# Gates, branch, output and down projections with the tokens stationary and 512 weight columns moving

## The chip, the cores and the metric

The kernel runs on one core of a Trainium2 chip. The metric is device time in microseconds (us); the figure quoted for a kernel is the median of its runs. A profile shows one execution, with the busy time of TensorE (PE, its weight loads apart as PEld), VectorE (DVE), ScalarE (ACT), GpSimd (POOL), and the queues that issue transfers (SP's above all).

## The reference

One encoder layer on 256 tokens, D = 2048, in float32. `setup_inputs` only draws values; the shapes are constants.

```python
h = rmsnorm(x, mix_norm)
z = h @ w_in                  # q/kv latents, rotary key, conv v/B/C, memory query, 3 x 2048 gates
y_mla  = mla_attention(...) @ w_o_mla            # 1024 -> 2048
y_conv = (cb * dwconv_centred(cc * cv, conv_w)) @ w_out_conv   # 1024 -> 2048
y_mem  = memory_attention(...) @ w_o_mem         # 1024 -> 2048
gates  = sigmoid(g + gate_bias)                  # (256, 3, 2048)
merged = gates[0] * y_mla + gates[1] * y_conv + gates[2] * y_mem
x = x + merged @ w_o                             # 2048 -> 2048
u = dwconv_centred(rmsnorm(x, ffn_norm) @ w_up, ffn_conv_w)    # 2048 -> 2 x 5632
a, b = split(u)
x = x + (silu(a) * b) @ w_down                   # 5632 -> 2048
return rmsnorm(x, final_norm)
```

## The kernel before

Every float32 operand of a product is cut into two float32r halves: `hi` is a rounded copy (made on ACT), `lo` the remainder (a subtraction on DVE). A product is three products: hi x hi, lo x hi and hi x lo. Weights come from memory in blocks of 128 x 2048 (1 MB; `load`, three buffers `raw`, issued on SP's queue), and `halves` (lines 138 and 139) makes `hi` (three buffers) and `lo` (two buffers) of each. All activations are kept features x tokens (feature-major) as tiles of 128 features x (256 hi | 256 lo).

There are two forms of a projection.

*The narrow form* (`mm`, `acc`, lines 161 to 165) has the weights stationary: a 128 x 128 piece of `hi` with the 512 columns hi|lo of the tokens moving, then a piece of `lo` with the 256 columns hi moving. One output tile is 128 output features x 256 tokens. Over 2048 input features that is 16 matmuls with 512 columns and 16 with 256. The second half of the result is added to the first afterwards by `total` (lines 185 and 187: one copy on ACT, one addition on DVE).

*The wide form* (`values`, lines 370 to 372, and `part`, lines 734 to 736) has the tokens stationary: 128 tokens of one feature tile, with 512 columns of `hi`, then of `lo` moving, then the tokens' lo half with `hi` moving. Its result is tokens x features. Before the change the value projections of the two attentions and the last 512 columns of the last down projection use it.

The stages in order: latents, keys, values and the two attentions with the gated convolution; then the merge (loop over `pair`: per pair of output tiles and per branch, two gate tiles and one block with two branch tiles of 8 input tiles each, `pair` 0 to 7); the output projection with the residual (`wo`, 16 tiles, which also makes the normalised input `h2` of the FFN); and twice (`NG`) `up` for 22 tiles of both halves of the FFN, with its convolution and gate, and `down` for 16 tiles (12 in the second round), each over 22 input tiles. At the end the last 512 columns are computed in the wide form, for one half of the tokens after the other, and `finish` normalises and stores each half; for that, part of the residual is turned by TensorE (line 724) and the factors are spread over partitions by a matmul with a diagonal (line 753).

The order of the instructions on each engine is made by the framework's scheduler from the program; each engine then runs its own list strictly in that order.

Of the kernel before, what the change touches and what calls it, by code (L numbers as in the profile page):

```python
# [64 lines left out]
TAIL = 4  # L65
LEAD = 5
# [5 lines left out]
OUT_SHAPE = (2, P, KC * P)  # L72
# [4 lines left out]
def tile_kernel(ctx: ExitStack, tc: tile.TileContext, a, out):  # L77
# [21 lines left out]
    def temp(name):  # L99
        tag, bufs = {"hl": ("hl", 2), "t": ("t", 3), "s": ("s", 2), "sq": ("sq", 3)}.get(name, ("w", 8))  # L100
        return tmp.tile([P, T], F32, tag=tag, name=name, bufs=bufs)
# [528 lines left out]
    mg = [slot(f"mg{i}", F32R) for i in range(KC)]  # L630
    for pair in range(KC // 2):
        ms_ = [None, None]
        for br, (w, src) in enumerate((("woa", oa), ("woc", yc), ("wom", om))):
            gs = []
            for j in range(2):
                hi, lo = wblock()
                t = total(mm(hi, lo, 0, xs))
                nc.vector.tensor_tensor(t, t, rsb, op=ALU.mult)
                g = temp(f"g{j}")
                nc.scalar.activation(g, t, AF.Sigmoid, bias=col("gb", br * KC + 2 * pair + j))  # L640
                gs.append(g)
            hi, lo = block(a[w][pair])
            for j in range(2):
                t = total(mm(hi, lo, j * 8 * P, src))
                if br == 0:
                    ms_[j] = temp(f"mg{j}")
                    nc.vector.tensor_tensor(ms_[j], t, gs[j], op=ALU.mult)
                else:
                    nc.vector.tensor_tensor(t, t, gs[j], op=ALU.mult)
                    nc.vector.tensor_tensor(ms_[j], ms_[j], t, op=ALU.add)  # L650
        for j in range(2):
            split(mg[2 * pair + j], ms_[j])


    x2 = [slot(f"xr{i}") for i in range(KC // 2)]
    h2 = []
    fsq = temp("sq")
    for i in range(KC):
        if i % 2 == 0:
            nc.sync.dma_start(x2[i // 2], a["xT"][:, i * T : (i + 2) * T])  # L660
        hi, lo = block(a["wo"][i])
        t = total(mm(hi, lo, 0, mg))
        x = half(x2[i // 2], i % 2)
        nc.vector.tensor_tensor(x, x, t, op=ALU.add)
        d = slot(f"h2_{i}", F32R)
        split(d, x, col("ffn", i))
        h2.append(d)
        square_sum(fsq, x, i == 0)
# [4 lines left out]
    def up(c):  # L673
        ps = [mm(*block(a["wup"][2 * c + part]), 0, h2) for part in range(2)]
        if not rfb:
            rfb.append(spread(norm_factor(fsq, D, "f"), half(fb, 0)))
        ab = []
        for part in range(2):
            t = total(ps[part])
            u = temp(f"u{part}")  # L680
            nc.vector.tensor_tensor(u, t, rfb[0], op=ALU.mult)  # L681
            v = temp(f"v{part}")
            conv(u, v, "fcw", part * NFF + c, 2 * NFF)
            ab.append(v)
        s = temp("si")
        nc.scalar.activation(s, ab[0], AF.Silu)
        nc.vector.tensor_tensor(s, s, ab[1], op=ALU.mult)  # L687
        f = slot(f"f{c}", F32R)
        split(f, s)
        return f  # L690

    osq = temp("sq")
    wdn = iter(range(a["wdn"].shape[0]))

    def down(fs, tiles, last):
        n = len(fs) // 2
        for i in range(tiles):
            ps = psum()
            for b in range(2):
                hi, lo = block(a["wdn"][next(wdn)], n=n * P)  # L700
                acc(ps, hi, lo, 0, fs[b * n : (b + 1) * n], b == 0, b == 1)
            x = half(x2[i // 2], i % 2)
            nc.vector.tensor_tensor(x, x, total(ps), op=ALU.add)
            if last:
                square_sum(osq, x, i == 0)
                nc.scalar.activation(x, x, AF.Copy, scale=col("fin", i))

    ready = []
    for g in range(NG):
        fs = ready + [up(c) for c in range(g * GF + len(ready), (g + 1) * GF)]  # L710
        ready = [up((g + 1) * GF)] if g < NG - 1 else []
        last = g == NG - 1
        down(fs, KC - TAIL if last else KC, last)

    gains = slot("gains")
    nc.scalar.dma_start(gains, a["fing"])
    rows = []
    for h in range(2):  # L720
        pt = atps.tile([P, 2 * T], F32, tag="at", name="ptr")
        for c in range(TAIL):
            src = half(x2[(KC - TAIL + c) // 2], c % 2)
            nc.tensor.transpose(pt[:, c * P : (c + 1) * P], src[:, h * P : (h + 1) * P], ident)
        rows.append(slot(f"rows{h}"))
        nc.scalar.activation(rows[h], pt, AF.Copy)
    rest = tiny.tile([P, 2], F32, tag="rest", name="rest")
    nc.vector.tensor_scalar(rest, feature_sums(osq), 1.0 / D, EPS, op0=ALU.mult, op1=ALU.add)
    po = [psum() for _ in range(2)]

    def part(h, c, hi, lo):
        f = fs[c]
        fh, fl = f[:, h * P : (h + 1) * P], f[:, T + h * P : T + (h + 1) * P]
        nc.tensor.matmul(po[h], fh, hi, start=c == 0, stop=False)  # L734
        nc.tensor.matmul(po[h], fh, lo, start=False, stop=False)  # L735
        nc.tensor.matmul(po[h], fl, hi, start=False, stop=c == GF - 1)  # L736

    left = (KC - TAIL) * P

    def finish(h):  # L740
        y, junk = slot(f"y{h}"), slot("junk")
        nc.vector.tensor_tensor(y, po[h], rows[h], op=ALU.add)
        m = tiny.tile([P, 2], F32, tag="om", name="om")
        nc.scalar.activation(junk, y, AF.Square, accum_out=m[:, 0:1])
        nc.vector.tensor_scalar(
            m[:, 1:2], m[:, 0:1], 1.0 / D, rest[:, h : h + 1], op0=ALU.mult, op1=ALU.add
        )
        r = tiny.tile([P, 1], F32, tag="or", name="or")
        nc.gpsimd.tensor_tensor(r, m[:, 1:2], mhalf[:, 0:1], op=ALU.pow)
        dg = tmp.tile([P, P], F32, tag="dg", name="dg")  # L750
        nc.vector.tensor_scalar(dg, ident, r, None, op0=ALU.mult)
        ps = atps.tile([P, 2 * T], F32, tag="at", name="pso")
        spread_in = nc.tensor.matmul(ps[:, 0:P], ones, dg, start=True, stop=True)
        res = raws.tile([P, WB], F32, tag="raw", name="res")
        g = slot(f"g{h}")
        nc.vector.tensor_tensor(g, y, gains, op=ALU.mult)
        nc.scalar.activation(res[:, left:], g, AF.Copy, scale=r)
        by = ps[:, 0:P].unsqueeze(1).to_broadcast([P, 2, P])
        for i in range((KC - TAIL) // 2):
# [6 lines left out]
            elif i == 0:  # L766
                nc.sync.dma_start(out[h][:, left:], res[:, left:])
# [3 lines left out]
    for b in range(0, GF, 4):  # L771
# [137 lines left out]
```

## Time and profile before

| | |
|---|---|
| median of 3 runs | 1642.61 us (1641.99 to 1644.32) |
| profiled execution, its own time | 1642.26 us |
| its span in the profile | 1640.5 us (1.76 us of the time lie around it) |
| PE busy | 1626.7 us, 99% of the span |
| PEld / DVE / ACT busy | 88% / 69% / 51% |
| chain that ended last | PE 98% |

A duration of one matmul is longer than the distance to the next, since matmuls overlap in the array. Where the time of a sequence of matmuls is wanted, it is read as the distance from start to start.

### The profile page before, as it was taken

To read this page: it belongs to the slowest core of one execution; us is meant where nothing else is said; L and a number is where in the kernel's file an instruction comes from. 1 tells how busy PE (TensorE), PEld (TensorE's weight loads), DVE (VectorE), ACT (ScalarE), POOL (GpSimd) and SP (SyncE) were. 2 spreads that over 40 slices of the span, in tenths; PEclk is the share of its full clock that TensorE was granted. 3 is DMA by queue.
4 is the path that set the end of the run, shared out by engine and by line. 5 is a ranking of instruction groups with operands and counts; after the bars stand their busy time and mean duration, and the time that the engine had idled before them with its cause. 6 is when DMAs were issued, how large, how long until landed. Compare 5 with 4: busy or idle time off the path is not lost.

```text
span 1640.5 us, 23631 instructions
## 1 busy us (share of the span) xinstructions
PE 1626.7 (99%) x9626; PEld 1447.5 (88%) x9626; DVE 1135.0 (69%) x1535; ACT 840.0 (51%) x1118; POOL 11.6 (1%) x23
## 2 busy tenths in 40 slices
PE   9999999999999999999999999999999999999997
PEld 8998888998888888888888888888888888888886
DVE  7756768776666666666676777778555778777554
ACT  8634545554544544444455655555444455554552
POOL 0000000000000000000000000000000000000000
PEclk9999999999999999999999999999999999999999
DMA  8555445444555455555465555554556555554563
GB/s 319 205 187 183 169 149 199 155 160 170 184 186 199 180 192 193 180 194 191 178 234 205 181 197 187 182 199 160 179 192 210 198 196 181 194 190 161 184 213 116
DMA packets 52443, 308.97 MB, mean 188 GB/s; under 512 B 6000, under 2 KB 7536, under 8 KB 22256
## 3 DMA queue, kind: packets, MB, share of 16 engines
q1 hardware_dynamic: 50688, 305.82, 52.1%
q8 instruction: 76, 1.25, 0.3%
q10 hardware_dynamic: 1008, 1.12, 0.2%
q0 software_dynamic: 640, 0.52, 0.2%
q14 instruction: 31, 0.25, 0.0%
HBM read 304.17 MB, written 2.10 MB: 187 GB/s over the span
## 4 chain that ended last, share of the span: by engine, by line
PE 98%; DMA 1%; DVE 1%; issue 0%; ACTq 0%; ACT 0%; SPq 0%; POOLq 0%; POOL 0%; DVEq 0%
PE ps L161 51%; PE ps L163 29%; PE ps L165 4%; PE ps L173 2%; PE ps L174 2%; PE ps L175 2%; PE ps L371 1%; PE ps L372 1%; PE ps L370 1%; PE pss L436 1%; PE ps L734 0%; PE ps L736 0%; PE ps L735 0%; DMA raw<-in_wkv 0%; PE pst L460 0%
## 5 line engine op out<-in xcount | busy, mean ns | idle before, releaser
L139 DVE TENSOR_TENSOR lo<-raw,hi 128x2048 fp32r<-128x2048 f32 (+2 forms) x312 | 649.3, 2083 | 346.0 <-PE ps L163 272.1
L161 PE MATMUL ps<-h,hi 128*128 128x512 f32 x2520 | 606.5, 391 | 2.1 <-DVE t L187 2.1
L138 ACT ACTIVATE hi<-raw 128x2048 fp32r<-128x2048 f32 (+2 forms) x312 | 543.1, 1743 | 63.4 <-PE ps L175 18.2
L161 PEld LDWEIGHTS ps<-h,hi 128*128 128x128 f32 x2520 | 471.4, 188 | 96.5 <-DVE t L187 2.3
L163 PEld LDWEIGHTS ps<-h,lo 128*128 128x128 f32 x2688 | 345.0, 191 | 13.0
L163 PE MATMUL ps<-h,lo 128*128 128x256 f32 x2688 | 350.2, 283 | 0.0
L185 ACT ACTIVATE hl<-ps 128x256 f32<-128x256 f32 x253 | 97.5, 385 | 432.9 <-PE ps L165 425.8
L161 PE MATMUL ps<-f,hi 128*128 128x512 f32 x588 | 144.0, 391 | 0.0
L161 PEld LDWEIGHTS ps<-f,hi 128*128 128x128 f32 x588 | 108.6, 188 | 20.8
L187 DVE TENSOR_TENSOR t<-ps,hl 128x256 f32<-128x256 f32 x253 | 105.8, 418 | 8.7 <-ACT hl L185 8.7
L163 PEld LDWEIGHTS ps<-f,lo 128*128 128x128 f32 x616 | 81.4, 191 | 4.4
L163 PE MATMUL ps<-f,lo 128*128 128x256 f32 x616 | 82.8, 282 | 0.0
L544 ACT ACTIVATE v<-u,taps 128x256 f32<-128x256 f32 x88 | 44.7, 510 | 70.5 <-DVE u L681 70.5
L545 DVE SCALAR_TENSOR_TENSOR v<-u,taps,v 128x255 f32<-128x255 f32 x88 | 42.5, 484 | 48.8 <-ACT v L544 48.8
L165 PE MATMUL ps<-h,hi 128*128 128x512 f32 x168 | 66.6, 396 | 0.0
L161 PE MATMUL ps<-mg,hi 128*128 128x512 f32 x240 | 57.3, 390 | 0.0
L161 PEld LDWEIGHTS ps<-mg,hi 128*128 128x128 f32 x240 | 45.1, 188 | 9.1
L194 ACT ACTIVATE f<-si 128x256 fp32r<-128x256 f32 x44 | 18.3, 417 | 53.7 <-DVE si L687 53.7
L548 DVE SCALAR_TENSOR_TENSOR v<-u,taps,v 128x255 f32<-128x255 f32 x88 | 42.5, 484 | 3.0
L681 DVE TENSOR_TENSOR u<-t,fb 128x256 f32<-128x256 f32 x88 | 37.3, 425 | 2.9
L174 PE MATMUL ps<-m,lo 128*128 128x256 f32 x128 | 35.9, 284 | 0.0
L175 PE MATMUL ps<-m,hi 128*128 128x256 f32 x128 | 35.9, 284 | 0.0
(247 smaller groups left out, 1635.5 us busy)
## 6 DMA issues: line engine op xcount, KB each, us to landing
raw<-in_wup SPq DMA_DIRECT2D x88, 1024.0 KB, 4.8
raw<-in_win SPq DMA_DIRECT2D x83, 1024.0 KB, 4.8
raw<-in_wdn SPq DMA_DIRECT2D x56, 704.0 KB, 4.0
raw<-in_wo SPq DMA_DIRECT2D x16, 1024.0 KB, 4.8
raw<-in_wmk SPq DMA_DIRECT2D x8, 1024.0 KB, 4.9
raw<-in_wmv SPq DMA_DIRECT2D x8, 1024.0 KB, 4.8
raw<-in_woa SPq DMA_DIRECT2D x8, 1024.0 KB, 4.8
raw<-in_woc SPq DMA_DIRECT2D x8, 1024.0 KB, 4.7
```

The source lines that it names most:

```text
L138: nc.scalar.activation(hi[:, s], raw[:, s], AF.Copy)
L139: nc.vector.tensor_tensor(lo[:, s], raw[:, s], f32(hi[:, s]), op=ALU.subtract)
L161: nc.tensor.matmul(ps, hi[:, ks[k]], xs[k], start=first and k == 0, stop=False)
L163: nc.tensor.matmul(ps[:, 0:T], lo[:, ks[k]], xs[k][:, 0:T], start=False, stop=False)
L165: nc.tensor.matmul(ps, hi[:, ks[k]], xs[k], start=False, stop=True)
L174: nc.tensor.matmul(p1, lo[:, s], x[:, 0:T], start=False, stop=False)
L175: nc.tensor.matmul(p1, hi[:, s], x[:, T:], start=False, stop=stop)
L185: nc.scalar.activation(hl, ps[:, T:], AF.Copy)
L187: nc.vector.tensor_tensor(t, ps[:, 0:T], hl, op=ALU.add)
L544: nc.scalar.activation(dst, x, AF.Copy, scale=col(w, wn + wi))
L545: nc.vector.scalar_tensor_tensor(dst[:, 1:T], x[:, 0 : T - 1], col(w, wi), dst[:, 1:T], op0=ALU.mult, op1=ALU.add)
L548: nc.vector.scalar_tensor_tensor(dst[:, 0 : T - 1], x[:, 1:T], col(w, 2 * wn + wi), dst[:, 0 : T - 1], op0=ALU.mult, op1=ALU.add,)
```

## The change

The gates, the three branch projections, the output projection and both rounds of the down projection go to the wide form, by `project` and `multiply`, in groups of 512 output columns (`NW` = 4 groups); `up` stays narrow. The merged sum and the residual are then tokens x features. The merged sum must be feature-major for the output projection, and the new residual for `up`: `turned` transposes four 128-column pieces of both token halves on TensorE (8 transposes), and splits them. It is called with a delay: it is put on the list `pending` and taken from it by `flush` 12 feature tiles into a later projection (for the last group of the residual: inside the first tile of `up`). `total` falls away in the changed projections; the gate bias is read from memory, spread over the tokens, by 12 transfers issued on ACT; the mean squares are sums along a row. `finish` scales by a number per token, with no matmul. The number of buffers for `raw`, `hi` and `lo` is as before.

```diff
+    def project(src, n, xs, hook=None):
+
+        ps = [psum() for _ in range(2)]
+        per = WB // 512
+        for b in range(0, len(xs), per):
+            cnt = min(per, len(xs) - b)
+            hi, lo = block(src[n][:, b * 512 : (b + cnt) * 512], n=cnt * 512)
+            for k in range(cnt):
+                if hook is not None and b + k == len(xs) - 4:
+                    hook()
+                for h in range(2):
+                    multiply(ps[h], xs[b + k], h, hi, lo, k, b + k == 0, b + k == len(xs) - 1)
+        return ps
+
+    def multiply(ps, x, h, hi, lo, k, first, final):
+        xh, xl = x[:, h * P : (h + 1) * P], x[:, T + h * P : T + (h + 1) * P]
+        s = slice(k * 512, (k + 1) * 512)
+        nc.tensor.matmul(ps, xh, hi[:, s], start=first, stop=False)
+        nc.tensor.matmul(ps, xh, lo[:, s], start=False, stop=False)
+        nc.tensor.matmul(ps, xl, hi[:, s], start=False, stop=final)
+
+    def turned(src, dst, gain=None):
+
+        for c in range(0, 4, 2):
+            pt = psum(atps, "at")
+            for j in range(2):
+                for h in range(2):
+                    o = j * T + h * P
+                    nc.tensor.transpose(
+                        pt[:, o : o + P], src[h][:, (c + j) * P : (c + j + 1) * P], ident
+                    )
+            for j in range(2):
+                split(dst[c + j], half(pt, j), None if gain is None else col("ffn", gain + c + j))
...
-    for pair in range(KC // 2):
-        ms_ = [None, None]
+    for n in range(NW):
+        ms_ = [slot(f"m{h}") for h in range(2)]
         for br, (w, src) in enumerate((("woa", oa), ("woc", yc), ("wom", om))):
+            bias = wide("bias")
+            nc.scalar.dma_start(bias, a["gb"][:, br * D + n * 512 : br * D + (n + 1) * 512])
+            gp = project(a["wg"], br * NW + n, xs, flush)
...
+            for h in range(2):
+                g = ms_[h] if br == 0 else wide("g")
+                nc.vector.scalar_tensor_tensor(
+                    g, gp[h], rs[:, h : h + 1], bias, op0=ALU.mult, op1=ALU.add
+                )
+                nc.scalar.activation(g, g, AF.Sigmoid)
                 gs.append(g)
...
+            bp = project(a[w], n, src)
+            for h in range(2):
+                nc.vector.tensor_tensor(gs[h], bp[h], gs[h], op=ALU.mult)
+                if br:
+                    nc.vector.tensor_tensor(ms_[h], ms_[h], gs[h], op=ALU.add)
+        pending.append(lambda ms_=ms_, n=n: turned(ms_, mg[4 * n : 4 * n + 4]))
...
+        ps = project(a["wo"], n, mg, flush)
+        for h in range(2):
+            x = x2[h][n]
+            nc.vector.tensor_tensor(x, ps[h], x, op=ALU.add)
+            squares(fst, x, h, n)
...
+            ps = project(a["wdn"], g * NW + n, fs)
+            for h in range(2):
+                x = x2[h][n]
+                nc.vector.tensor_tensor(x, ps[h], x, op=ALU.add)
...
+        for i in (0, n, 1, 2):
+            s = slice(i * 512, (i + 1) * 512)
+            if i in (0, 1):
+                nc.scalar.activation(res[:, s], x2[h][i], AF.Copy, scale=r)
+            else:
+                nc.vector.tensor_scalar(res[:, s], x2[h][i], r, None, op0=ALU.mult)
+            (nc.sync if i in (n, 2) else nc.scalar).dma_start(out[h][:, s], res[:, s])
```

The built programs show where the instructions then stand. Up to the end of the gated convolution, the lists of PE, DVE and ACT are the same in both, but for the line numbers. Three places follow; the numbers behind a name tell buffers apart.

PE, out projection, from one output tile to the next before the change (`ps_7895` and `ps_7945` are the results, `mg` the merged sum):

```order
L163 MATMUL ps_7895<-mg13_4289,lo_7892 128x256
L163 MATMUL ps_7895<-mg14_4290,lo_7892 128x256
L163 MATMUL ps_7895<-mg15_4291,lo_7892 128x256
L165 MATMUL ps_7895<-mg15_4291,hi_7891 128x512
L161 MATMUL ps_7945<-mg0_4276,hi_7941 128x512
L161 MATMUL ps_7945<-mg1_4277,hi_7941 128x512
```

And after it, where the third weight block of the first group ends (`ps_6717`, `ps_6718`: first group, token halves 0 and 1; `ps_6865`, `ps_6866`: second group; `m0`, `m1`: the merged sum, tokens x features):

```order
L653 MATMUL ps_6718<-hi_6781,mg11_4287 128x512
L662 MATMUL ps_6815<-ident_85,m1_6087 128x128
L662 MATMUL ps_6824<-ident_85,m0_6086 128x128
L662 MATMUL ps_6824<-ident_85,m1_6087 128x128
L662 MATMUL ps_6824<-ident_85,m0_6086 128x128
L662 MATMUL ps_6824<-ident_85,m1_6087 128x128
L651 MATMUL ps_6865<-hi_6869,mg0_4276 128x512
L651 MATMUL ps_6866<-hi_6869,mg0_4276 128x512
L652 MATMUL ps_6865<-lo_6870,mg0_4276 128x512
```

Between the third and the fourth block of the first group now stand five transposes and most of the first block of the second group (20 matmuls, up to `mg3`), and then the fourth block with `mg12`; so two blocks are open at once.

PE, some 40 instructions on, where the fourth block of the first group ends and the rest of the second group's first block follows:

```order
L653 MATMUL ps_6718<-hi_6811,mg15_4291 128x512
L653 MATMUL ps_6865<-hi_6869,mg3_4279 128x512
L651 MATMUL ps_6866<-hi_6869,mg3_4279 128x512
L652 MATMUL ps_6866<-lo_6870,mg3_4279 128x512
L653 MATMUL ps_6866<-hi_6869,mg3_4279 128x512
L651 MATMUL ps_6865<-hi_6899,mg4_4280 128x512
L651 MATMUL ps_6866<-hi_6899,mg4_4280 128x512
L662 MATMUL ps_6963<-ident_85,x20_6690 128x128
L662 MATMUL ps_6972<-ident_85,x20_6690 128x128
L652 MATMUL ps_6865<-lo_6900,mg4_4280 128x512
```

The first matmul that needs the second block's `lo_6900` now stands eight instructions behind the end of the fourth block.

DVE, merge, before the change (`lo` is the weights' lower half, `t` a narrow tile's sum, `g` a gate):

```order
L139 TENSOR_TENSOR lo_4731<-raw_4728,hi_4730 128x2048
L187 TENSOR_TENSOR t_4667<-ps_4632,hl_4665 128x256
L638 TENSOR_TENSOR t_4667<-t_4667,rsb_567 128x256
L187 TENSOR_TENSOR t_4697<-ps_4678,hl_4695 128x256
L649 TENSOR_TENSOR t_4697<-t_4697,g0_4624 128x256
L650 TENSOR_TENSOR mg0_4411<-mg0_4411,t_4697 128x256
L139 TENSOR_TENSOR lo_4777<-raw_4774,hi_4776 128x2048
```

And after it, around the end of a gate projection (`ps_4488`, `ps_4489`) and of the branch projection behind it (`ps_4616`, `ps_4617`):

```order
L685 SCALAR_TENSOR_TENSOR g_4610<-ps_4488,xr_565,bias_4486 128x512
L143 TENSOR_TENSOR lo_4651<-raw_4648,hi_4650 128x2048
L685 SCALAR_TENSOR_TENSOR g_4613<-ps_4489,xr_565,bias_4486 128x512
L143 TENSOR_TENSOR lo_4689<-raw_4686,hi_4688 128x2048
L692 TENSOR_TENSOR g_4610<-ps_4616,g_4610 128x512
L143 TENSOR_TENSOR lo_4719<-raw_4716,hi_4718 128x2048
L692 TENSOR_TENSOR g_4613<-ps_4617,g_4613 128x512
L694 TENSOR_TENSOR m0_4292<-m0_4292,g_4610 128x512
L694 TENSOR_TENSOR m1_4293<-m1_4293,g_4613 128x512
```

An eviction that waits for the end of a projection now stands directly ahead of the `lo` of a block that PE needs later.

DVE, the end of the kernel for the first half of the tokens, before the change:

```order
L742 TENSOR_TENSOR y0_15151<-ps_14990,rows0_14976 128x512
L756 TENSOR_TENSOR g0_15164<-y0_15151,gains_14969 128x512
L745 TENSOR_SCALAR om_15154<-om_15154,rest_14985 128x1
L751 TENSOR_SCALAR dg_15159<-ident_85,or_15157 128x128
L762 TENSOR_TENSOR res_15163<-xr0_7780,pso_15161 128x256
L762 TENSOR_TENSOR res_15163<-xr1_7781,pso_15161 128x256
```

After it:

```order
L787 TENSOR_TENSOR x20_6693<-ps_13016,x20_6693 128x512
L790 TENSOR_SCALAR om_13187<-ost_7307,oe_13013 128x1
L796 TENSOR_TENSOR x20_6693<-x20_6693,gains_7311 128x512
L803 TENSOR_SCALAR res_13192<-x20_6692,or_13189 128x512
L803 TENSOR_SCALAR res_13192<-x20_6693,or_13189 128x512
```

Of six products of 128 x 256 behind the factor, two of 128 x 512 are left on DVE; two more stand on ACT, each half's last two transfers behind them.

## Rows read from the trace of the kernel before

**Rows 1.** The page's first part (busy time of each engine, share of the span, instructions) and its part 4 (the chain that ended last, by engine).

```profile
PE 1626.7 (99%) x9626; PEld 1447.5 (88%) x9626; DVE 1135.0 (69%) x1535; ACT 840.0 (51%) x1118; POOL 11.6 (1%) x23
...
PE 98%; DMA 1%; DVE 1%; issue 0%; ACTq 0%; ACT 0%; SPq 0%; POOLq 0%; POOL 0%; DVEq 0%
```

**Rows 2.** Windows by stage: start and end, length, then busy time of each engine with its instructions, granted clock of PE, busy share of the DMA engines, GB/s. In order: merge, output projection, first `down`, second `down`, last 512 columns, what follows the last matmul.

```profile
404.17:805.45 401.28, 401.28 (x2306) 354.16 (x2304) 259.48 (x312) 196.70 (x233) 0.00 (x0) 1.00 0.52 188
805.45:894.49 89.04, 89.04 (x514) 78.71 (x512) 61.73 (x81) 47.73 (x63) 0.00 (x0) 1.00 0.59 213
...
1151.48:1274.15 122.67, 122.67 (x706) 108.20 (x705) 66.49 (x68) 50.73 (x51) 0.00 (x0) 1.00 0.56 192
...
1507.95:1600.85 92.90, 92.90 (x538) 81.98 (x537) 54.55 (x62) 47.65 (x63) 0.00 (x0) 1.00 0.56 193
1600.85:1631.72 30.87, 30.87 (x139) 25.26 (x137) 15.79 (x23) 9.71 (x14) 0.55 (x1) 1.00 0.31 114
1631.72:1640.50 8.78, 0.49 (x3) 0.30 (x2) 3.96 (x10) 1.44 (x3) 0.55 (x1) 0.77 0.36 134
```

**Rows 3.** Waits of DVE and of SP's queue: engine, line, for whom, us in total, times, longest.

```profile
DVE lo L139 <- PE ps L163: 272.1, 233, 4.6
...
SPq L129 <- DVE lo L139: 1063.7, 206, 10.0
```

**Rows 4.** Timeline of PE, one narrow tile over 16 input tiles and the start of the next: start, us from first start to last end, line, operation, count.

```profile
1279.71 3.58 PE L161 MATMUL ps<-h,hi 128*128 128x512 f32 x15
1283.13 2.08 PE L163 MATMUL ps<-h,lo 128*128 128x256 f32 x16
1285.05 0.40 PE L165 MATMUL ps<-h,hi 128*128 128x512 f32 x1
1285.28 1.09 PE L161 MATMUL ps<-h,hi 128*128 128x512 f32 x4
```

**Rows 5.** Timeline of PE in the wide form (`values`): one weight block, 24 matmuls from the first row to the last but one; then four matmuls with 128 columns stand in between. The last row is from the groups by line, the weight loads of line 371: count, busy us, mean ns.

```profile
135.26 0.61 PE L370 MATMUL ps<-hi,m 128*128 128x512 f32 x2
135.72 0.39 PE L371 MATMUL ps<-lo,m 128*128 128x512 f32 x1
...
140.48 0.39 PE L372 MATMUL ps<-hi,m 128*128 128x512 f32 x1
140.70 0.61 PE L370 MATMUL ps<-hi,m 128*128 128x512 f32 x2
...
L371 PEld LDWEIGHTS ps<-lo,m 128*128 128x128 f32 x64 | 12.0, 188 | 2.4
```

**Rows 6.** Timeline of PE with four transposes (line 460) among the 15 hi matmuls of a narrow tile, and the source view of line 460 (duration ns, lowest, median, highest).

```profile
200.06 2.00 PE L161 MATMUL ps<-h,hi 128*128 128x512 f32 x8
201.90 0.27 PE L460 MATMUL pst<-ident,p 128*128 128x128 f32 x1
...
202.71 0.49 PE L460 MATMUL pst<-ident,p 128*128 128x128 f32 x3
...
203.96 2.08 PE L163 MATMUL ps<-h,lo 128*128 128x256 f32 x16
...
L460 PE MATMUL pst<-ident,p x48: 270/272/275, 186.2 to 395.7; 128*128 128x128 f32 x48
```

**Rows 7.** Timeline of PE around the two other kinds of small matmul that fall away: the column sums of the squares (line 221; one more matmul with 512 columns follows ahead of the next row) and the spreading of the factor (line 753; likewise).

```profile
1609.25 0.39 PE L735 MATMUL ps<-lo,f 128*128 128x512 f32 x1
1609.48 0.50 PE L221 MATMUL psm<-ones,sq 128*128 128x1 f32 x4
...
1610.17 0.40 PE L734 MATMUL ps<-hi,f 128*128 128x512 f32 x1
...
1627.67 0.39 PE L736 MATMUL ps<-wh,f 128*128 128x512 f32 x1
1627.89 0.38 PE L753 MATMUL pso<-dg,ones 128*128 128x128 f32 x2
...
1628.35 0.39 PE L735 MATMUL ps<-wl,f 128*128 128x512 f32 x1
```

**Rows 8.** Groups by line and shape on DVE and ACT: count, busy us, mean ns of one, idle time before them.

```profile
L139 DVE TENSOR_TENSOR lo<-raw,hi 128x2048 fp32r<-128x2048 f32 x238 | 545.3, 2291 | 253.4 <-PE ps L163 208.3 <-issue 15.3 <-PE ps L174 13.3
L742 DVE TENSOR_TENSOR y<-ps,rows 128x512 f32<-128x512 f32 x2 | 1.4, 691 | 10.6 <-PE ps L736 10.6
L138 ACT ACTIVATE hi<-raw 128x2048 fp32r<-128x2048 f32 x238 | 454.7, 1911 | 42.7 <-PE ps L175 18.2 <-PE ps L372 17.8 <-DVE lo L139 5.4
```

**Rows 9.** Timeline of all engines after the last matmul (PEld left out).

```profile
1631.33 0.39 PE L736 MATMUL ps<-wh,f 128*128 128x512 f32 x1
1631.76 0.69 DVE L742 TENSOR_TENSOR y<-ps,rows 128x512 f32<-128x512 f32 x1 [1.37 <-PE ps L736]
...
1633.53 0.55 POOL L749 TENSOR_TENSOR or<-om,mhalf 128x1 f32<-128x1 f32 x1 [6.29 <-DVE om L745]
...
1634.12 0.72 ACT L757 ACTIVATE res<-g,or 128x512 f32<-128x512 f32 x1 [0.91 <-POOL or L749]
...
1634.87 0.33 SPq L767 DMA_DIRECT2D out<-res  x1
...
1635.76 1.66 SPq L765 DMA_DIRECT2D out<-res  x3
```

**Rows 10.** DMA issues by line: count, KB each, median us from issue to landing.

```profile
raw<-in_win SPq DMA_DIRECT2D x83, 1024.0 KB, 4.8
```

More of the change, by code (lines that the diff above doesn't have):

```diff
@@ L642, in tile_kernel @@
[L642 to L652, printed above, removed]
@@ L690, in up @@
         return f
[L692 to L706, printed above, removed]
@@ L708, in tile_kernel @@
-    ready = []
+    ost = const.tile([P, 2 * NW], F32, name="ost")
+    gains = [slot("gains") for n in range(NW)]
     for g in range(NG):
-        fs = ready + [up(c) for c in range(g * GF + len(ready), (g + 1) * GF)]
-        ready = [up((g + 1) * GF)] if g < NG - 1 else []
+        fs = [up(c) for c in range(g * GF, (g + 1) * GF)]
         last = g == NG - 1
[L713 to L728, printed above, removed]
@@ L729, in tile_kernel @@
-    po = [psum() for _ in range(2)]
[L731 to L738, printed above, removed]
+        if last:
+            for n in range(NW):
+                nc.scalar.dma_start(gains[n], a["fing"][:, n * 512 : (n + 1) * 512])
@@ L740, in finish @@
+        for n in range(NW - last):
+            ps = project(a["wdn"], g * NW + n, fs)
+            for h in range(2):
+                x = x2[h][n]
+                nc.vector.tensor_tensor(x, ps[h], x, op=ALU.add)
+                if last:
+                    squares(ost, x, h, n)
+                    nc.vector.tensor_tensor(x, x, gains[n], op=ALU.mult)
+    n = NW - 1
+    rest = mean_square(ost, "o", NW - 1)
+    po = [psum() for _ in range(2)]
     def finish(h):
-        y, junk = slot(f"y{h}"), slot("junk")
@@ L803, in _rows @@
+            continue
+        for k in range(cnt):
+            hi, lo = slot("wh", F32R), slot("wl", F32R)
+            piece = raw[:, k * 512 : (k + 1) * 512]
+            nc.scalar.activation(hi, piece, AF.Copy)
+            nc.vector.tensor_tensor(lo, piece, f32(hi), op=ALU.subtract)
+            late.append((b + k, hi, lo))
+    for h in range(2):
+        for k, hi, lo in late:
+            multiply(po[h], fs[k], h, hi, lo, 0, False, k == GF - 1)
+        finish(h)
 def _rows(w):
@@ L841, in _layout @@
         order += [o_c + part * CW + i * P + r(P) for part in (0, 2, 1)]
-    for pair in range(KC // 2):
-        order += [o_g + br * D + 2 * pair * P + r(2 * P) for br in range(3)]
     h = r(HEADS)[:, None]
```

190 lines of the change are left out of this document (86 added, 104 removed).

## The prediction

> **What bounds the kernel now.** I read the page's first part and the chain of waits first: PE is busy for 99% of the span and holds 98% of the chain that ended last [rows 1]. Then the windows by stage, since the change touches some stages and not others: from the merge to the last matmul PE is busy for the whole of every stage, at the full granted clock, 2.4 GHz [rows 2]. The waits say the same from the other side: DVE stands 272.1 us waiting for PE to release a `lo` buffer, and SP's queue 1063.7 us for DVE [rows 3]. So the weights arrive and are split ahead of need, and the time is a sum over PE's instructions. What must be known is the distance from start to start of a matmul in each form, and whether PE still never waits.
>
> **What a matmul costs.** A narrow tile over 16 input tiles, 16 matmuls with 512 and 16 with 256 columns, takes 1285.28 - 1279.71 = 5.57 us [rows 4], 348 ns for a 128 x 128 piece of weights. In the wide form 24 matmuls with 512 columns take 140.70 - 135.26 = 5.44 us, 226.7 ns each [rows 5]. They cover four input tiles and four output tiles, 16 pieces, so 340 ns a piece. The columns that move are the same, 768 a piece. The 16 matmuls with 256 columns take (1285.05 - 1283.13) / 16 = 120 ns each [rows 4]. So 256 columns more make 106.7 ns, and 13.3 ns a matmul are left that don't grow with its columns. A narrow piece pays them twice and a wide one 1.5 times; the change between the two kinds in a narrow tile costs a little more. That is the gain: 8 ns a piece.
>
> The tokens' half stands still for two matmuls in turn in the wide form, but it is loaded each time: line 371 has 64 weight loads for its 64 matmuls [rows 5]. They take 188 ns, less than the 226.7 ns between matmuls, so no more comes from there.
>
> **The change part by part**, against the profiled execution (1642.26 us, of which 1640.5 are span; the median, 1642.61, is 0.35 above).
>
> *Matmuls.* Merge: 4 groups x 3 branches x (16 + 8) input tiles x 6 = 1728 matmuls, x 226.7 ns = 391.7 us, where it takes 401.28: -9.6. Output projection: 384, 87.0 us, for 89.04: -2.0. First `down`: 4 x 22 x 6 = 528, 119.7, for 122.67: -3.0. Second `down`, its first three groups: 396, 89.8, for 92.90: -3.1; the 8 transposes of line 724 stand in that window and go with it [rows 2]. The last 512 columns have that form already, `up` keeps its own. Together -17.7.
>
> *Small matmuls taken out.* Four instructions of line 221, for one column sum: from 1609.25 to 1610.17, two wide matmuls (0.45) and 0.47 us for them; two such sums fall away. The spreading of the factor in the stream: 1628.35 - 1627.67 - 0.45 = 0.23 [rows 7]. Together -1.2.
>
> *Transposes put in.* 64, eight for each of four groups of the merged sum and of the residual. Four among 15 hi matmuls make 3.90 us (200.06 to 203.96) [rows 6], where such 15 take 3.42 (1283.13 - 1279.71) [rows 4]: 0.12 us each, +7.7. The Trainium skill, "TensorE: Matmul & The Clock Gate", Part 4 (PE-mode transpose), gives about 275 ns for a transpose of 128 x 128 in a kernel. The trace agrees with that as a duration, 272 ns, but not as a price, since the next matmul starts earlier [rows 6]; at 275 ns each the 64 would cost 17.6, and nearly the whole gain would be gone.
>
> *Stalls put in.* `lo` has two buffers. In the regular course DVE writes the `lo` of the block after next when a block ends: 2.29 us [rows 8], and PE needs it 5.44 us later; an eviction of 0.69 us ahead of it leaves 2.4 us. That hides the evictions of 128 x 512 everywhere in the merge. In the half blocks that end each `down` projection, two input tiles, 2.72 us, no eviction stands between and 0.4 us are left. The one place where it does not fit is the first group of the output projection. PE must wait for the merged sum's last transposes, and the scheduler has put the second group's first block in between. When the third block ends, that block's `lo` only gets its buffer: ready after 2.29 us, while PE has five transposes (0.6) and two matmuls (0.45): +1.25. When the fourth block ends, the second block's `lo` again starts only then, and PE has six matmuls and two transposes, 1.6 us: +0.7. At the first tile of `up`, which needs the last eight transposes, the scheduler gives PE some 20 hi matmuls of two tiles (4.6 us) and 12 lo ones ahead of the first of them that need the second token half; the eviction, one `lo` and the second eviction (0.69 + 2.29 + 0.69 = 3.7) end before. For what I overlook there and in the half blocks, +0.5. Bounds: 0 if all is hidden; above, the rival on DVE. Taken: +2.4.
>
> *The end.* Up to the factor (1634.08) nothing is shorter. Then 3.3 us pass until the last transfer is issued (1637.42) [rows 9]. Afterwards ACT scales two pieces of 128 x 512 (0.72 each) and issues two transfers (0.33 each), 2.1 us; DVE's two are not longer, by the 0.69 of an addition of that size [rows 8, 9]. -1.2, between 0 and -2.
>
> *At nothing:* ACT and DVE lose `total` on 140 narrow tiles and gain evictions; neither bounds (DVE 259 of the merge's 401 us, ACT 197) [rows 2]. Bias, gains and residual add 3.75 MB to transfers that keep the DMA engines 52 to 59% busy [rows 2]. A weight block is now 128 rows of 8 KB that don't lie next to one another in memory; it lands in 4.8 us now [rows 10] and is needed every 5.44, with three buffers. If the rows came half as fast, that cover would be gone.
>
> Sum: -17.7 - 1.2 + 7.7 + 2.4 - 1.2 = -10.0, so 1632.3 for such an execution and 1632.6 for the median.
>
> **The rivals.**
>
> *The eviction ahead of `lo` decides (no change or slower).* DVE runs in order, and `L685`, `L692`, `L720` and `L774` wait for the end of a projection with a `lo` behind them. There are 35 such ends (24 in the merge, 4, 4 and 3). If ACT's split, or the wait for a transfer, came 2.4 us late too, the slack would be used up, and from there each end costs what is missing. From 10.0 / 35 = 0.29 us an end the gain is gone; at 0.7 us each it is 1647. For it: these waits are new, and no row shows how they fall. Against: DVE now spends 272 us waiting for PE [rows 3].
>
> *The wide matmul is no cheaper by the column (slower).* If the 226.7 ns held only in the short stretches where they were seen, and in a long one each cost what a narrow piece's columns cost, 348 x 512 / 768 = 232 ns, the 3036 matmuls would give back 16: 1649. It decides from 230 ns. Against: the 30.87 us of the last 512 columns, 132 such matmuls, contain 29.9 us at 226.7 and the small ones [rows 2, 7]. The Trainium skill, "TensorE: Matmul & The Clock Gate", section "Back-to-back issue gap", has N / 2.4 + 2.5 ns, which leaves next to nothing to save by wider matmuls. The trace disagrees, with 13 ns in place of 2.5 [rows 5].
>
> *A transpose costs its whole duration (no change).* 64 x (272 - 120) = +9.7: 1642. Against: 3.90 us with four of them [rows 6].
>
> *The rows of the weight blocks come slowly (slower).* In the merge a block of 5.57 us keeps the DMA engines busy for 52% [rows 2, 4], 2.9 us; at half the rate it would be 5.8 instead of the 5.44 that PE needs: +0.36 on 130 blocks, 47 in all, 1679. Against: no row shows a slow transfer of rows of that size.
>
> *All stalls hidden, end at its lower bound (faster still):* 1629.
>
> **How the numbers follow.** Differences under 0.2% (3.3 us) can't be told from none here. Forecast with its bounds, 1629 to 1637: 0.76. Eviction rival: 0.12, of which 0.04 ends above 1646. Column rival: 0.04. Transposes: 0.05. Slow rows: 0.03. Faster: 0.76 and the part of the eviction rival below 1639, 0.03: 0.79. Slower: 0.04 + 0.04 + 0.03 = 0.11. Same: 0.10. The range reaches from 1629 to 1641, which adds the mild half of the eviction rival.
>
> **What would show it.** Right: PE over 98% busy; starts 226.7 ns apart in lines 651 to 653; the merge in 394 to 395 us; 8 transposes in 1 us; PE waits of 0.7 to 1.3 us for `lo` in the output projection and hardly any others; the last transfer issued some 2 us after the factor. Wrong: a wait of PE for line 143 at each end of a projection, a distance of 230 ns or more, or SP's queue no longer waiting for DVE.

## The result, and the profile after

The changed kernel takes 1634.99 us (median of 5 runs, 1633.71 to 1636.67) where the kernel before takes 1642.66 beside it: ratio 0.995, 95% interval 0.9935 to 0.9964. That is 7.7 us less; 10.0 were forecast. The executions of either kernel lie up to 3 us apart, so stages are compared in the profiled ones: 1633.83 us with a span of 1632.0, against 1642.26 and 1640.5, 8.5 us less by span.

The lines of the code moved: line 133 loads a block, 142 and 143 split it into hi and lo, 165 to 169 are the narrow form, 651 to 653 the wide one, 662 the transposes, 720 the out projection's eviction, 787 to 804 the end. The page's first part and its chain by engine answer to [rows 1]:

```profile
PE 1615.9 (99%) x8658; PEld 1400.2 (86%) x8658; DVE 1054.7 (65%) x1270; ACT 786.9 (48%) x931; POOL 12.4 (1%) x23
...
PE 98%; DVE 1%; issue 0%; DMA 0%; ACT 0%; ACTq 0%; POOLq 0%; POOL 0%; DVEq 0%
```

PE still sets the time, with 968 instructions fewer. The windows by stage, cut at the first matmul of each, have the columns of [rows 2]; merge and output projection are one window here, since the scheduler interleaves them:

```profile
403.90:892.00 488.10, 486.19 (x2169) 401.80 (x2168) 259.00 (x191) 198.92 (x155) 0.00 (x0) 1.00 0.58 200
892.00:1138.39 246.39, 246.39 (x1421) 217.72 (x1421) 193.16 (x269) 139.96 (x183) 0.71 (x1) 1.00 0.52 187
1138.39:1258.10 119.71, 119.71 (x530) 99.10 (x529) 56.96 (x37) 43.92 (x27) 0.00 (x0) 1.00 0.53 188
1258.10:1503.01 244.91, 244.91 (x1410) 216.46 (x1408) 191.92 (x261) 136.09 (x173) 0.00 (x0) 1.00 0.53 192
1503.01:1592.79 89.78, 89.78 (x398) 74.33 (x396) 45.74 (x33) 35.89 (x29) 0.00 (x0) 1.00 0.57 197
1592.79:1622.87 30.08, 30.08 (x133) 24.59 (x131) 15.23 (x23) 10.87 (x19) 0.93 (x1) 1.00 0.34 119
1622.87:1632.00 9.13, 0.00 (x0) 0.00 (x0) 2.39 (x5) 2.06 (x4) 0.93 (x1) 0.72 0.37 127
```

and the two `up` stages of before, which no row has shown yet:

```profile
894.49:1151.48 256.99, 256.99 (x1481) 227.22 (x1480) 200.32 (x278) 140.62 (x185) 0.71 (x1) 1.00 0.51 185
...
1274.15:1507.95 233.80, 233.80 (x1346) 206.64 (x1345) 182.46 (x249) 126.33 (x165) 0.00 (x0) 1.00 0.52 188
```

The `up` stages are to be read together: before the change two tiles of the second stood in the first's window (1481 matmuls there, 1421 after). In us, with the forecast put together from the prediction's terms:

| stage | before | after | measured change | forecast change |
|---|---|---|---|---|
| up to the merge | 404.17 | 403.90 | -0.3 | 0 |
| merge, output projection | 490.32 | 488.10 | -2.2 | -2.9 (matmuls -11.6, 56 transposes +6.7, two waits +1.95) |
| both `up`, both `down` | 706.36 | 700.79 | -5.6 | -5.1 (matmuls -6.1, 8 transposes +1.0, unknown +0.5, a column sum -0.5) |
| last 512 columns | 30.87 | 30.08 | -0.8 | -0.7 (a column sum, the factor's matmuls) |
| after the last matmul | 8.78 | 9.13 | +0.35 | -1.2 |

The stages with matmuls come out as they were added up, within 0.7 us each. The last line has the wrong sign, and its 1.55 us are as much as the 1.5 us by which the profiled execution misses the forecast; the other lines miss by -0.5 to +0.7 and nearly cancel.

The waits of PE for line 143, of DVE for the wide matmuls, and of SP's queue (engine, line, for whom, us in total, times, longest), against [rows 3]:

```profile
PE ps L652 <- DVE lo L143: 1.9, 2, 1.2
...
DVE lo L143 <- PE ps L652: 190.7, 62, 4.2
...
SPq L133 <- DVE lo L143: 1337.1, 257, 13.0
```

DVE still waits for PE, and SP's queue more than before. PE waits for `lo` twice, and the timeline of PE shows where (start, us, line, operation; in brackets the wait and its releaser):

```profile
809.88 0.49 PE L662 MATMUL ps<-ident,m 128*128 128x128 f32 x3
810.13 0.49 PE L652 MATMUL ps<-lo,mg 128*128 128x512 f32 x1
...
815.26 0.71 PE L662 MATMUL ps<-ident,m 128*128 128x128 f32 x5
815.72 0.71 PE L651 MATMUL ps<-hi,mg 128*128 128x512 f32 x2
817.63 0.50 PE L652 MATMUL ps<-lo,mg 128*128 128x512 f32 x1 [1.19 <-DVE lo L143]
...
828.65 0.38 PE L662 MATMUL ps<-ident,x 128*128 128x128 f32 x2
829.75 0.50 PE L652 MATMUL ps<-lo,mg 128*128 128x512 f32 x1 [0.72 <-DVE lo L143]
```

Five transposes and two hi matmuls, then 1.19 us of nothing; at the second group's second block 0.72. The forecast had 1.25 and 0.7 at these two places.

The end, in the timeline of all engines (PEld left out), against [rows 9]; behind it the landing of the output transfers (count, KB each, us from issue to landing): first the last four after the change, in order, each from a window that holds one issue, then the median before:

```profile
1622.48 0.39 PE L653 MATMUL ps<-wh,f 128*128 128x512 f32 x1
...
1624.39 0.21 DVE L790 TENSOR_SCALAR om<-ost,oe 128x1 f32<-128x1 f32 x1 [0.79 <-ACT junk L704]
1624.52 0.68 DVE L796 TENSOR_TENSOR x<-x,gains 128x512 f32<-128x512 f32 x1
1624.68 0.93 POOL L795 TENSOR_TENSOR or<-om,mhalf 128x1 f32<-128x1 f32 x1 [5.87 <-DVE om L790]
1625.65 1.33 ACT L801 ACTIVATE res<-x,or 128x512 f32<-128x512 f32 x2 [1.29 <-POOL or L795]
...
1626.16 0.81 SPq L804 DMA_DIRECT2D out<-res  x2
1626.40 0.95 ACTq L804 DMA_DIRECT2D out<-res  x2
```

```profile
out<-res SPq DMA_DIRECT2D x1, 256.0 KB, 2.4
out<-res ACTq DMA_DIRECT2D x1, 256.0 KB, 3.0
out<-res SPq DMA_DIRECT2D x1, 256.0 KB, 3.6
out<-res ACTq DMA_DIRECT2D x1, 256.0 KB, 3.8
```

```profile
out<-res SPq DMA_DIRECT2D x8, 256.0 KB, 2.3
```

The factor stands at 1624.68 + 0.93 = 1625.61, the last issue ends at 1626.40 + 0.95 = 1627.35, 1.74 us later; before it took 3.34 [rows 9]. That is the gain that was forecast, 1.6 us. But from there to the end of the span are 4.65 us, where it was 1640.50 - 1637.42 = 3.08: 1.57 us given back. And from the last matmul to the factor there are 2.74 us for 2.36, since POOL's power takes 0.93 instead of 0.55. -1.60 + 1.57 + 0.38 = +0.35.

The four transfers are issued 0.2 to 0.4 us apart now, and were issued 0.7 to 0.9 us apart before. Yet they land at 1628.6, 1629.4, 1630.2 and 1630.9, and landed at 1637.2, 1638.0, 1638.7 and 1639.5 before: 0.7 to 0.8 us apart in both kernels.

### The profile page after: what moved, and what is told of

Same layout as the page of the kernel before. It is cut to its first block, busy times and chain, and to the rows that moved or that the text cites. A ratio compares the mean times of both kernels' runs of the same rounds, so it can differ in the third digit from the quotient of the medians.

```text
span 1632.0 us, 21129 instructions
## 1 busy us (share of the span) xinstructions
PE 1615.9 (99%) x8658; PEld 1400.2 (86%) x8658; DVE 1054.7 (65%) x1270; ACT 786.9 (48%) x931; POOL 12.4 (1%) x23
## 4 chain that ended last, share of the span: by engine, by line
PE 98%; DVE 1%; issue 0%; DMA 0%; ACT 0%; ACTq 0%; POOLq 0%; POOL 0%; DVEq 0%
PE ps L165 25%; PE ps L652 15%; PE ps L653 14%; PE ps L651 14%; PE ps L167 14%; PE ps L177 2%; PE ps L178 2%; PE ps L179 2%; PE ps L169 2%; PE ps L375 1%; PE ps L376 1%; PE ps L374 1%; PE pss L440 1%; DVE lo L143 1%; PE ps L662 0%
## 5 line engine op out<-in xcount | busy, mean ns | idle before, releaser
L165 PE MATMUL ps<-h,hi 128*128 128x512 f32 x1785 | 431.4, 391 | 2.0 <-DVE t L191 2.0
L165 PEld LDWEIGHTS ps<-h,hi 128*128 128x128 f32 x1785 | 333.2, 188 | 68.5 <-DVE t L191 2.3
L167 PEld LDWEIGHTS ps<-h,lo 128*128 128x128 f32 x1904 | 244.5, 191 | 9.4 <-DVE lo L143 0.2
L167 PE MATMUL ps<-h,lo 128*128 128x256 f32 x1904 | 248.5, 283 | 0.0
L652 PE MATMUL ps<-lo,h 128*128 128x512 f32 x384 | 149.7, 390 | 0.0
L653 PE MATMUL ps<-hi,h 128*128 128x512 f32 x384 | 149.5, 389 | 0.0
L651 PE MATMUL ps<-hi,h 128*128 128x512 f32 x384 | 142.6, 390 | 0.0
L653 PE MATMUL ps<-hi,f 128*128 128x512 f32 x332 | 129.2, 389 | 0.0
L652 PE MATMUL ps<-lo,f 128*128 128x512 f32 x332 | 129.1, 389 | 0.0
L651 PE MATMUL ps<-hi,f 128*128 128x512 f32 x332 | 123.3, 389 | 0.0
L653 PEld LDWEIGHTS ps<-hi,h 128*128 128x128 f32 x384 | 72.1, 188 | 15.0
L651 PEld LDWEIGHTS ps<-hi,h 128*128 128x128 f32 x384 | 72.1, 188 | 14.8
L653 PEld LDWEIGHTS ps<-hi,f 128*128 128x128 f32 x332 | 62.3, 188 | 13.0
L651 PEld LDWEIGHTS ps<-hi,f 128*128 128x128 f32 x332 | 62.3, 188 | 12.9
```

The lines of the kernel that those rows point to most:

```text
L165: nc.tensor.matmul(ps, hi[:, ks[k]], xs[k], start=first and k == 0, stop=False)
L167: nc.tensor.matmul(ps[:, 0:T], lo[:, ks[k]], xs[k][:, 0:T], start=False, stop=False)
L651: nc.tensor.matmul(ps, xh, hi[:, s], start=first, stop=False)
L652: nc.tensor.matmul(ps, xh, lo[:, s], start=False, stop=False)
L653: nc.tensor.matmul(ps, xl, hi[:, s], start=False, stop=final)
```

## The experiments

The theory is the prediction's: a matmul costs its columns and 13.3 ns, a transpose in the stream 0.12 us, evictions are hidden, the two waits come from two open blocks on two `lo` buffers. For the end: POOL is slowed by DVE's multiplication beside it, and four transfers issued together land late. The rivals are those on record. Medians in us, beside runs of the kernel before on the same chip (one chip for e0, e2, e4 and e5, a second for e1, e3, e6 and e7, a third for e8):

| kernel | median | before | ratio, 95% interval |
|---|---|---|---|
| e0_after | 1634.54 | 1642.67 | 0.9951 [0.9939, 0.9964] |
| e2_turn_twice | 1640.01 | 1642.67 | 0.9988 [0.9979, 0.9998] |
| e4_early_turn | 1631.73 | 1642.67 | 0.9936 [0.9924, 0.9949] |
| e5_gains_first | 1634.01 | 1642.67 | 0.9947 [0.9935, 0.996] |
| e1_cols256 | 1673.53 | 1641.74 | 1.0191 [1.0172, 1.0209] |
| e3_evict6 | 1633.71 | 1641.74 | 0.9951 [0.9936, 0.9967] |
| e6_quarter_out | 1632.06 (one run) | 1641.74 | - |
| e7_both | 1631.42 | 1641.74 | 0.9937 [0.9925, 0.9949] |
| e8_cols384 | 1825.33 | 1642.58 | 1.1114 [1.1081, 1.1146] |

**The base.** 

> The changed kernel again, unaltered, as the base for the three others on the same chip. Expected 1633.7 to 1636.7 us, and 7.0 to 8.5 us under the kernel before.

8.1 us under the kernel before, as expected; its span is 1632.7.

**Half as wide matmuls.** In `multiply`:

```diff
-        s = slice(k * 512, (k + 1) * 512)
-        nc.tensor.matmul(ps, xh, hi[:, s], start=first, stop=False)
+        for c in range(0, 512, 256):
+            s, p = slice(k * 512 + c, k * 512 + c + 256), ps[:, c : c + 256]
+            nc.tensor.matmul(p, xh, hi[:, s], start=first and c == 0, stop=False)
...
```

> Each wide matmul with 512 columns (3036 in gates, branches, output and down projections, 132 in the last 512 columns) is issued as two with 256 columns; the columns that move stay the same. If 13.3 ns of a matmul don't depend on its columns, the 3168 additional ones cost 42 us: about 1677 us, and in the trace starts 120 ns apart. If the time goes by columns alone, as the rival on the wide matmul has it, nothing is added: about 1635 us and starts 113 ns apart.

39.0 us more than e0_after, 12.3 ns for each additional matmul. Not all of that is matmuls: PE's two waits for `lo` are gone here, and one of 1.2 us for the split of a turned tile has come. From the first matmul of `up` to the last of the kernel PE waits in neither kernel (columns as in [rows 2]; first e0_after, then this kernel):

```profile
892.73:1623.55 730.82, 730.82 (x3885) 632.34 (x3883) 502.86 (x619) 366.45 (x431) 1.64 (x2) 1.00 0.52 188
917.91:1662.79 744.88, 744.88 (x4942) 687.55 (x4940) 503.42 (x619) 366.22 (x431) 1.64 (x2) 1.00 0.54 184
```

The 1056 additional ones there (528, 396 and 132) cost 14.06 us, 13.3 ns each. The timeline of PE in the merge:

```profile
409.82 0.28 PE L653 MATMUL ps<-lo,h 128*128 128x256 f32 x1
...
411.98 0.28 PE L653 MATMUL ps<-lo,h 128*128 128x256 f32 x1
```

There are 18 distances in 2.16 us, 120 ns each. The rival that goes by columns alone is out. The Trainium skill, "TensorE: Matmul & The Clock Gate", section "Back-to-back issue gap", gives N / 2.4 + 2.5 ns for a matmul by itself; an estimate from it is some 8 us more for the 3168 additional matmuls. The runs disagree, with 39.0.

Two sizes don't show a fixed part, though. 120 ns could as well be the least distance between two matmuls that each load weights.

**Three quarters and one quarter.** The same edit with 384 and 128 columns:

```diff
-        for c in range(0, 512, 256):
+        for c, w in ((0, 384), (384, 128)):
...
```

> Each wide matmul with 512 columns is issued as one with 384 and one with 128 columns, in rows of three of a kind. Two sizes in the runs so far (120 ns for 256 columns, 226.7 for 512) can't tell whether 120 is 256 columns and a fixed part, or a least distance that weight loads set. If every matmul costs 0.417 ns a column and 13.3 ns, a 384 takes 173 and a 128 takes 67 ns, 240 a pair as with 256 and 256: 1673.5 us as that kernel. If 128 columns take as long as 256 because the weight load sets the distance, a pair takes 173 + 120 = 293 ns, 66 ns more than one matmul with 512: 3168 x 66 = 210 us more, about 1844 us. If a 384 takes less than 165 ns, the fixed part isn't there and the 120 ns were the least distance all along.

190.8 us more than e0_after. One turn of three and three in its timeline:

```profile
419.98 0.40 PE L652 MATMUL ps<-hi,h 128*128 128x384 f32 x1
420.21 0.34 PE L653 MATMUL ps<-lo,h 128*128 128x384 f32 x1
420.38 0.34 PE L654 MATMUL ps<-hi,h 128*128 128x384 f32 x1
420.56 0.22 PE L652 MATMUL ps<-hi,h 128*128 128x128 f32 x1
420.62 0.27 PE L653 MATMUL ps<-lo,h 128*128 128x128 f32 x1
420.73 0.28 PE L654 MATMUL ps<-hi,h 128*128 128x128 f32 x1
420.84 0.39 PE L652 MATMUL ps<-hi,h 128*128 128x384 f32 x1
```

From 420.21 to 420.56 two matmuls with 384 columns take 0.35 us, 175 ns each. 120, 175 and 226.7 ns for 256, 384 and 512 columns lie on one line, 0.417 ns a column and 13 to 15 ns beside them. So the fixed part is there, and 120 ns was no least distance. Whether it belongs to the matmul or to its weight load no run tells, since every matmul has one. With 128 columns more is paid than the line gives: a whole turn takes 0.86 us, less 3 x 175 leaves 112 ns for each, not 67. That is a mean. The starts of a turn are not even: the first 128 stands only 60 ns ahead of the second, the other two 110, and the first 384 behind them takes 230. So what the small ones owe falls in part on the next wide one. That each of these matmuls has a weight load makes the load the likely limit; no run changed the load alone. The Trainium skill, "TensorE: Matmul & The Clock Gate", section "LDWEIGHTS (loading the stationary operand)", has a load take its columns / 1.2 ns; an estimate from it is 107 ns for 128 columns, which is near the mean of 112 in the trace, while the loads' own durations are listed with 187 to 192 ns.

**Transposes twice.** In `turned`, ahead of `nc.tensor.transpose`:

```diff
+                    for _ in range(2):
```

> Each of the 64 transposes of the merged sum and of the residual is issued twice. If a transpose in a stream of matmuls costs 0.12 us, 64 more cost 7.7 us: the gain over the kernel before falls to about nothing (ratio 0.9995 to 1.001). If it costs its whole duration of 272 ns, they cost 17.4 us, and the kernel is some 9 us slower than before. In the trace eight wide matmul intervals and transposes in a row show which: 16 transposes between two matmuls take 1.9 us or 4.4 us.

5.5 us more than e0_after, by medians and by span (1638.2 against 1632.7): less than the theory's 7.7, and the rival's 17.4 is far. Twelve of the transposes in a row, and PE's waits:

```profile
903.06 1.47 PE L663 MATMUL ps<-ident,x 128*128 128x128 f32 x12
904.29 1.87 PE L165 MATMUL ps<-h,hi 128*128 128x512 f32 x7
```

```profile
PE ps L652 <- DVE lo L143: 0.8, 2, 0.5
```

The twelve take 1.47 us to the end of the last, which lasts 0.27: they start (1.47 - 0.27) / 11 = 0.109 us apart, and 64 x 0.109 = 7.0. The two waits fall from 1.9 to 0.8 us, since the additional transposes stand where PE waited. 7.0 - 1.1 = 5.9; the 0.4 us to the measured 5.5 lie ahead of the merge, where the edit changes nothing and this execution is that much shorter. Their duration stays 272 ns; as a price in a stream that is 2.5 times too much.

**Seven evictions for one.** At the gate's eviction of token half 0:

```diff
-                nc.vector.scalar_tensor_tensor(
+                for _ in range(7 if h == 0 else 1):
+                    nc.vector.scalar_tensor_tensor(
...
```

> At each of the 12 gate projections of the merge DVE evicts the first token half seven times instead of once: six more instructions of 0.69 us, 4.1 us of DVE each time, which the scheduler puts three by three ahead of two blocks' lo. My theory: a block leaves 5.44 - 2.29 = 3.15 us of DVE to spare, three evictions take 2.1, so nothing or at most 0.4 us an end is added: 1634 to 1640 us, no waits of PE for lo in the merge. If evictions lie on the path (the first rival), 12 x 4.1 = 50 us are added: 1685 us, with a wait of PE for lo at each gate.

No more time than the changed kernel. Two rows of its evictions among DVE's groups in the merge (count, busy us, mean ns, idle before), and PE's wait for `lo` in the changed stages:

```profile
L686 DVE SCALAR_TENSOR_TENSOR g<-ps,xr,bias 128x512 f32<-128x512 f32 x64 | 47.2, 749 | 25.9 <-PE ps L653 24.7
L686 DVE SCALAR_TENSOR_TENSOR m<-ps,xr,bias 128x512 f32<-128x512 f32 x32 | 23.6, 749 | 5.5 <-PE ps L653 4.9
```

```profile
PE ps L652 <- DVE lo L143: 1.9, 2, 1.2
```

There are 96 evictions where there were 24, 54 us of work more, and PE has the same two waits, both in the output projection. The rival that puts evictions ahead of `lo` on the path is out with a wide margin.

**The last transposes four tiles earlier.** `project` gets the place of its hook as an argument:

```diff
-                if hook is not None and b + k == len(xs) - 4:
+                if hook is not None and b + k == len(xs) - at:
...
-        ps = project(a["wo"], n, mg, flush)
+        ps = project(a["wo"], n, mg, flush, 8 if n == 0 else 4)
```

> The first group of the output projection issues the last eight transposes of the merged sum four input tiles earlier, so that its fourth block follows its third and no block of the second group stands open between them. If the two waits of PE for lo (1.19 and 0.72 us) come from two blocks being open at once with two lo buffers, both go and the kernel takes 1.9 us less than the changed one; the stage from the merge to the end of the output projection takes 486.2 instead of 488.1 us. If they come from the transposes themselves (their split on ACT and DVE being late), waits of the same size stand at the first matmul that reads the turned tiles, and the time stays.

2.8 us less than e0_after, by medians and by span. The list of PE's waits has no line 652 any more. The window from the merge to the end of the output projection:

```profile
404.30:889.90 485.60, 485.60 (x2169) 401.88 (x2168) 259.09 (x191) 199.20 (x155) 0.00 (x0) 1.00 0.58 201
```

488.13 in e0_after, so 2.5 us go here. 1.9 are the waits. The other 0.6 are in PE's busy time, 486.22 to 485.60 for the same instructions. They belong to the waits too, since a wait is listed from the end of what stood before it. From start to start the first gap in the changed kernel is 817.63 - 816.04 = 1.59 us where 0.227 is usual, the second 0.99 us behind a transpose where 0.03 is usual: 2.3 us. And after the wait of 1.19 us the next matmul starts 0.33 us later and the following ones 0.23 to 0.24 us, instead of 0.227. So a wait costs more than its listed length. A third `lo` buffer, which would test the cause from the other side, was not run. The prediction's terms without waits give 391.7 + 87.0 + 56 x 0.12 = 485.4, within 0.2 of what is now there.

**Gains ahead of the factor.** In `finish`, with `z` scaled in place of `y`:

```diff
+        z = wide("z")
+        nc.vector.tensor_tensor(z, y, gains[n], op=ALU.mult)
         m = tiny.tile([P, 1], F32, tag="om", name="om")
...
-        nc.vector.tensor_tensor(y, y, gains[n], op=ALU.mult)
```

> The multiplication by the gains at the end goes into a tile of its own and runs while ACT takes the squares, ahead of the row factor and not beside it. If POOL's power took 0.93 instead of 0.55 us because DVE worked beside it, it falls back to 0.55 and the end, from the last matmul to the end of the span, is 0.4 us shorter (8.75 instead of 9.13). If the 0.93 us belong to POOL itself, both stay. The time as a whole moves by less than runs differ, so the trace decides.

As the theory has it:

```profile
1624.62 0.69 DVE L790 TENSOR_TENSOR z<-x,gains 128x512 f32<-128x512 f32 x1
...
1625.67 0.55 POOL L797 TENSOR_TENSOR or<-om,mhalf 128x1 f32<-128x1 f32 x1 [6.25 <-DVE om L792]
```

DVE's multiplication now runs beside ACT's squares, and the power takes 0.55 us again. The Trainium skill, "SBUF — State Buffer", section "SBUF: two separate sides", says that DVE and GpSimd share a pair of ports that one of them holds for a whole instruction, a DVE instruction with two inputs in SBUF among them. The trace agrees in kind: the multiplication is not longer beside the power (0.68 us) than here (0.69), and the power is by 0.38. But the power did not wait for the whole multiplication and then take its 0.55: in the changed kernel it ended 1625.61 - 1625.20 = 0.41 us behind it. It was not tried with a DVE instruction with one input.

The end, from the last matmul (1623.86) to the end of the span (1632.7), takes 8.84 us, where e0_after has 9.15. The medians differ by 0.5, less than the executions do.

**A quarter of the last transfers.** In `finish`, ahead of the transfer:

```diff
+            if h == 1:
+                s = slice(i * 512, i * 512 + 128)
```

> Of the second token half, each of the four output transfers at the end writes 128 of its 512 columns, 64 KB in place of 256; the rest of these rows is left unwritten. If the last transfers land late (3.0 to 3.4 us after their issue) because 1 MB is under way at once, they land in at most 2.3 us and the span ends some 1.3 us sooner after the last issue (3.1 to 3.4 us instead of 4.65). If it is the queues or the number of transfers, both stay.

This kernel leaves three quarters of the second half's output unwritten. The last four issues, and the landing of the small transfers (the first token half's still have 256 KB):

```profile
1626.54 0.81 SPq L806 DMA_DIRECT2D out<-res  x2
1626.78 0.95 ACTq L806 DMA_DIRECT2D out<-res  x2
```

```profile
out<-res SPq DMA_DIRECT2D x2, 256.0 KB, 3.1
out<-res ACTq DMA_DIRECT2D x2, 256.0 KB, 3.4
out<-res SPq DMA_DIRECT2D x2, 64.0 KB, 1.7
out<-res ACTq DMA_DIRECT2D x2, 64.0 KB, 1.7
```

The order and the distances of the issues are the same; with 64 KB they land in 1.7 us on either queue, and the span ends 1630.2 - 1627.73 = 2.5 us after the last issue instead of 4.65. So it is the bytes, not the queues and not the number of transfers. Both the bytes of the transfer itself and those ahead of it count: the first of the four takes 2.4 us with 256 KB, the last 3.8.

**Both.** The edits of e4 and e5 in one kernel. 

> The early transposes and the gains multiplied ahead of the factor in one kernel: 2.8 and 0.4 us under the changed kernel if both gains add, 1631.3 us, ratio to the kernel before 0.993. If one of them hides the other, 1631.7.

The lowest median, 1631.42, but not to be told from e4's: their ratios are 0.9937 and 0.9936. In the trace both gains are there (no wait of PE for `lo`; the power 0.55 us; the end 8.83 us). It takes 10.3 us less than the kernel before on its chip, where e0_after takes 8.1 less on its own: 2 to 3 us less than the changed one.

## Why the prediction was right, and where it was not

*Matmuls, -17.7.* Right. First `down` 119.71 and second 89.78 us were forecast as 119.7 and 89.8. e1 and e8 show the reason: a part of 13 to 15 ns that doesn't depend on the columns, paid 1.5 times a piece instead of twice. The rival on columns needed 230 ns a matmul; 226.7 held over whole stages.

*Transposes, +7.7.* Right. One more in a row costs 0.11 us (e2); the price of 0.12 also holds what the matmuls around a row lose, the first behind it above all (0.32 instead of 0.227 us to the next). The sum of the stage agrees with 0.12 (e4).

*Stalls, +2.4.* The two waits in the output projection are where they were put, 1.19 and 0.72 us for 1.25 and 0.7, and e4 shows the cause by removing them. The 0.5 for what might be overlooked elsewhere was not needed, since PE waits for `lo` at no other place in the changed stages. What was overlooked is that a wait costs more than its listed length, 2.5 us for the two (e4). That the whole term, 2.4, comes so near is luck: the spare 0.5 stood for another thing.

*Evictions at nothing.* Right; e3 shows that even six more at a gate find room. The slow weight rows did not come either: the median of landing of gate, output and `down` blocks is 4.7 to 4.8 us, that of the branches' blocks 5.0 to 5.1 where it was 4.7 to 4.8, and PE waits for none of them.

*The end, -1.2.* This step failed: "Afterwards ACT scales two pieces of 128 x 512 (0.72 each) and issues two transfers (0.33 each), 2.1 us". That the issues end sooner was right, 1.74 us after the factor. But the sum put the time from the last issue to the end of the span at no change, without a reason; it went from 3.08 to 4.65 us. Before, the issues were spread over 1634.87 to 1637.42, and the first was landing when the last was issued; now 1 MB is issued between 1626.16 and 1627.35, and the transfers still land 0.7 to 0.8 us apart. From the factor to the end of the span are 6.4 us in both kernels (1640.50 - 1634.08, 1632.0 - 1625.61). e6 shows that the bytes set it. To that came 0.38 us on POOL, which the words "Up to the factor (1634.08) nothing is shorter" allowed no loss for, though the change moved DVE's multiplication by the gains beside POOL's power. The bounds of this term, 0 and -2, did not hold the +0.35.

What is left between the 8.5 us by span and the 7.7 by medians is within the scatter of the executions; the other runs of the unaltered kernel give 8.1. The time still lies in the range, 1629 to 1641, since a miss of 1.55 us at the end is small against its 12.

## To carry to other kernels

When PE sets the time, count matmuls as columns plus a fixed part, and read both from stretches with two or three widths; a wider moving side then pays, until evictions or transposes take it back, and their price is the distance between starts, not the duration in the list. Where a change opens two weight blocks at once, count the buffers of what is made last for a block. At the end of a kernel the issue of the last transfer is not the end: here 1 MB could only leave after one late number, the transfers landed at the same pace however they were issued, and issuing them faster brought nothing. Read the landings one by one before a gain is put on the issues. And a listed wait of TensorE is counted from the end of the matmul before; its price is the distance from start to start.

## What the runs showed of the hardware beyond that

- POOL's power of 128 x 1 took 0.55 us alone and 0.92 to 0.93 us in every run in which DVE multiplied 128 x 512 beside it (0.68 us).
- At the end of the kernel four output transfers of 256 KB issued within 1.2 us landed in 2.4, 3.0, 3.6 and 3.8 us (in e1 and e8 in 2.0 to 3.2; why is not known); spread over 2.55 us, in 2.2 to 2.4; with 64 KB, in 1.7. With 256 KB they landed 0.6 to 0.8 us apart in all of these.
- Matmuls with 128 columns that each load weights, in rows of three between rows of three with 384, cost about 112 ns each: their starts stand 60, 111 and 112 ns ahead of the next, and the first wide one behind them takes 54 ns more. Transposes of that size stand 109 ns apart.
- After a wait or some transposes the first matmul takes 0.31 to 0.34 us to the next, and some of the ten behind it 0.23 to 0.24 instead of 0.227, at a granted clock of 1.00. Why stays open.
